# Two f32r matmul halves in one 512-column matmul, and bias loads for v placed further back

## The chip, the cores and the metric

The kernel runs on one core of one Trainium2 chip. The core's engines work side by side: TensorE (PE, with the loads of its stationary operand shown as PEld), VectorE (DVE), ScalarE (ACT), GpSimd (POOL) and SyncE (SP), which here only issues DMAs. Each engine carries out its own instructions in order, and semaphores tie the engines together. The metric is device microseconds of one execution; lower is better.

## The reference

`x` has 256 tokens and 2048 features, float32. A gMLP layer is followed by an attention layer:

```
h = x @ w_in + b_in                      # 2048 x 12288
u, v, g = split(h, 3)                    # 4096 columns each
v = layer_norm(gelu(v)) * vln_g + vln_b
mixed = einsum(causal w_s, v) + b_s      # per 128-token chunk and group of 512
x = layer_norm(ALPHA * x + (gelu(u) * mixed * silu(g)) @ w_out)

k, v = split(x @ kv_w, 2)                # 16 heads of 128
q, gate = split(x @ bw_in, 2)
weights = stick_breaking(q, k)           # strictly causal, in log space
x = layer_norm(ALPHA * x + ((weights @ v) * silu(gate)) @ bw_out)
```

## The kernel before

All products keep float32 accuracy with float32r operands: each operand is split into a high part (a cast on ACT, L89) and a low part (a subtraction on DVE, L90), and `mm3` (L98) adds three matmuls, high by high (L99), high by low (L100) and low by high (L101).

Weights arrive from HBM in chunks of 256 rows by 512 columns (`load_chunk`, L124, 512 KB, issued on SP at L128): six raw buffers (`wraw`), then five buffers each for the high and low parts (`wspl`, `WB = 5`). The order of the instructions on each engine is made by a planner that goes through the program by priority and by its own estimate of when each operand is there; `order(a, b)` fixes that b is issued after a.

**The v part of layer 1** (L385 to L434). v has eight groups of 512 columns. Groups 0 and 1 go through `gemm`. Groups 2 to 7 go in pairs (n = 2, 4, 6) through `bias_block` and `block` (L222), a list of steps from `plan` (L42): products named P1, Q5, P2, P6, P7, Q3, Q4 on sums of quarters, and twelve whole chunks, in the order P1, Q5, P2, chunk, P6, chunk, U3, P7, chunk, chunk, Q3, chunk, chunk, chunk, Q4, five chunks. Counted from 0, step 13 is the seventh chunk and step 14 is Q4. After some steps the accumulated product is added to a tile (`snap`, L321) that starts as a bias broadcast over 128 partitions: `bias_tile` (L378) issues two loads of 256 KB on SP, so that a pair of groups has four. These loads are written at the head of the loop for the pair before (L415). After the loop, `wsr` (the spatial weights, 512 KB) is loaded on SP (L429), masked on POOL (L430) and split on ACT and DVE (L432). The first use of its parts is in the blocks for u and g (L483), whose bias tiles are loaded on POOL's queue (L485).

**Layer 2** (L713). For each j of 4 (four heads each), `gemm` makes v with tokens as rows, 512 columns wide. Then three calls of `gemm_T` make k, q and the gate transposed, with the weight as stationary operand and x as moving one: for each of eight chunks, for each of four heads and two k, three matmuls of 256 columns. Two heads share a PSUM bank; at the end two instructions per bank evacuate it: `split` for k, L726 and L727 for q, Silu (L744) for the gate. Between q and gate, `scores` (L663) makes the logits; `hook` puts the cumulative sums (`weights`, L682) for the first two heads at chunk 3 of the gate's `gemm_T`, and for the other two at chunk 5. `weighted` (L697) follows. PSUM has four banks with the tag `acc` and four with `aux`; the small scratch tiles (`scratch`, L633) come from a pool of three.

Of the kernel before, what the change touches and what calls it, by code (L numbers as in the profile page):

```python
# [9 lines left out]
F32 = mybir.dt.float32  # L10
F32R = mybir.dt.float32r
# [20 lines left out]
WB = 5  # L32
HPINS = {6: (0, 1)}
TAIL = 7
HEAD = 7
ACT_M = (1, 3)
PINS = {4: (0, 1), 5: (2, 3)}
# [4 lines left out]
def plan(nk, hooks={}):  # L42


    each = (nk - 2 * NP) // CK
    steps = ["P1", "Q5", "P2", 1, "P6", 1, "U3", "P7", 1, 1, "Q3"] + [1] * (each - 4) + [0, "Q4"] + [0] * (each - 1)
    return [x for i, s in enumerate(steps) for x in [s, *hooks.get(i, ())]]
# [3 lines left out]
def trunk_kernel(ctx, tc, x, xT, w_in, b_in, vln_g, vln_b, w_sT, b_sT, w_out, kv_w, bw_in, bw_out, ln_g, ln_b, ln_gT, ln_bT, out):  # L51
# [14 lines left out]
    def nm(s):  # L66
        uid[0] += 1
        return f"{s}_{uid[0]}"

    def big_tile(shape, dt, s):  # L70
        return big.tile(shape, dt, tag="big", name=nm(s))
# [16 lines left out]
    def split(hi, lo, src):  # L88
        h = nc.scalar.copy(hi, src)  # L89
        return h, nc.vector.tensor_tensor(out=lo, in0=src, in1=hi.bitcast(F32), op=ALU.subtract)  # L90

    def order(*ins):
        for a, b in zip(ins, ins[1:]):
            tc.add_manual_dep(b.ins, a.ins.name,
                              mybir.DependencyInfo(mybir.DependencyClass.NoSync, mybir.DependencyReason.DATA),
                              reason="issue order")

    def mm3(acc, ah, al, bh, bl, start, stop, **kw):  # L98
        first = nc.tensor.matmul(acc, lhsT=ah, rhs=bh, start=start, stop=False, **kw)  # L99
        nc.tensor.matmul(acc, lhsT=ah, rhs=bl, start=False, stop=False, **kw)  # L100
        nc.tensor.matmul(acc, lhsT=al, rhs=bh, start=False, stop=stop, **kw)  # L101
        return first

    lead.tile([P, P // 8], F32, name="pad")
    xTh = lead.tile([P, KD, S], F32R, name="xTh")
    xTl = lead.tile([P, KD, S], F32R, name="xTl")
    ident = lead.tile([P, P], F32, name="ident")
    ntri = lead.tile([P, P], F32R, name="ntri")
    nones = lead.tile([P, P], F32R, name="nones")
# [14 lines left out]
    def load_chunk(wv, c, col0, spill=False, ahead=None):  # L124
        r = wraw.tile([P, CK, NT], F32, tag="raw", name=nm("raw"))
        src = wv[:, c * CK : (c + 1) * CK, col0 : col0 + NT]
        if not ahead:
            last_w[:] = [nc.sync.dma_start(r, src)]  # L128
        if spill:
            wh, wl = big_tile([P, CK, NT], F32R, "wh"), big_tile([P, CK, NT], F32R, "wl")  # L130
        else:
            wh = wspl.tile([P, CK, NT], F32R, tag="wh", name=nm("wh"))
            wl = wspl.tile([P, CK, NT], F32R, tag="wl", name=nm("wl"))
        if ahead:
            steps = []
            for j in range(CK):
                x_split = ahead(j - CK)
                nc.sync.dma_start(r[:, j, :], src[:, j, :])
                steps += [split(wh[:, j, :], wl[:, j, :], r[:, j, :]), x_split]
            for engine in zip(*steps):  # L140
                order(*engine)
        else:
            split(wh, wl, r)
        return wh, wl
# [174 lines left out]
    def bias_block(w, cols, nk, stat, forms, p, plan, dst, then):  # L319

        def snap(name, acc):  # L321
            d = dst(*dict(P1=(0, 0), Q5=(1, 1), P6=(0, 1), P7=(1, 1))[name])
            snapped[:] = [nc.vector.tensor_tensor(out=d, in0=d, in1=acc, op=ALU.add if name in ("P1", "Q5") else ALU.subtract)]

        def final(tok, half, acc):
            d = dst(tok, half)
            nc.vector.tensor_tensor(out=d, in0=d, in1=acc, op=ALU.add)
            then(tok, half)

        block(w, cols, nk, stat, forms, p, plan, snap, final)  # L330
# [44 lines left out]
        else:  # L375
            load_xT(c * CK, (c + 1) * CK, nc.sync)

    def bias_tile(s, c, q):  # L378
        t = big_tile([P, NTOK, NT], F32, s)
        for tok in range(NTOK):  # L380
            q.dma_start(t[:, tok, :], b_in[c : c + NT].partition_broadcast(P))
        return t


# [2 lines left out]
    for n in range(2):  # L387
# [19 lines left out]
        if n == 0:  # L407
            ahead_v = [bias_tile("v", AW + (n + i) * NT, nc.sync) for i in range(2, 4)]
            xforms = a_forms(xTh[:, 0 : 2 * NP, :], xTl[:, 0 : 2 * NP, :], NP)

    for n in range(2, G, 2):
        pair = ahead_v
        vt += pair
        if n + 2 < G:
            ahead_v = [bias_tile("v", AW + (n + i) * NT, nc.sync) for i in range(2, 4)]  # L415

        def v_then(tok, half, pair=pair, n=n):
            d = pair[1 - half][:, tok, :]
            nc.scalar.activation(d, d, AF.Gelu_apprx_tanh)
            nc.vector.bn_stats(vstats[:, tok, n + 1 - half, :], d)  # L420

        bias_block(w_in, (AW + (n + 1) * NT, AW + n * NT), KD, xstat, xforms, NP, plan(KD),
                   lambda tok, half, pair=pair: pair[1 - half][:, tok, :], v_then)


    wsh = big_tile([P, G, P], F32R, "wsh")
    wsl = big_tile([P, G, P], F32R, "wsl")
    wsr = big_tile([P, G, P], F32, "wsr")
    nc.sync.dma_start(wsr, w_sT.rearrange("g s t -> s g t"))  # L429
    nc.gpsimd.affine_select(out=wsr, in_=wsr, pattern=[[0, G], [1, P]], base=0, channel_multiplier=-1,  # L430
                            compare_op=ALU.is_ge, fill=0.0)
    split(wsh, wsl, wsr)  # L432
    bs = const.tile([P, G], F32, name="bs")
    nc.sync.dma_start(bs, b_sT)  # L434

# [205 lines left out]

    sps, wts = [], []

    def gemm_T(w, col0, evac, hook=None):
        accs = [ps_acc.tile([P, NT], F32, tag="acc", name=nm("acc")) for _ in range(2)]
        wv = w.rearrange("(k p) n -> p k n", p=P)
        for c in range(KD // CK):
            wh, wl = load_chunk(wv, c, col0)
            first = None
            for i in range(HPT):  # L650
                o = accs[i // 2][:, (i % 2) * S : (i % 2 + 1) * S]
                for j in range(CK):
                    k = c * CK + j
                    cs = slice(i * P, (i + 1) * P)
                    m = mm3(o, wh[:, j, cs], wl[:, j, cs], xTh[:, k, :], xTl[:, k, :],
                            start=(k == 0 and i % 2 == 0), stop=(k == KD - 1), **kw)
                    first = first or m
            if hook:
                hook(c, first)
        for i in range(2):  # L660
            evac(slice(2 * i, 2 * i + 2), accs[i].rearrange("p (h t) -> p h t", h=2))

    def scores(i, qT, kT):  # L663
        (qh, ql), (kh, kl) = qT, kT
# [48 lines left out]
    for j in range(4):  # L713
        v = big_tile([P, NTOK, NT], F32R, "avh"), big_tile([P, NTOK, NT], F32R, "avl")
        gemm(kv_w, D + j * NT, KD, xstat, lambda tok, acc, v=v: split(v[0][:, tok, :], v[1][:, tok, :], acc),
             head=HEAD if j == 0 else 0, after=anchor)
        if j == 0:
            sps += [padded("sph"), padded("spl")]
            wts += [(padded("wth"), padded("wtl")) for _ in range(HPT // 2)]
        kT = big_tile([P, HPT, S], F32R, "kTh"), big_tile([P, HPT, S], F32R, "kTl")  # L720
        gemm_T(kv_w, j * NT, lambda i, acc, kT=kT: split(kT[0][:, i, :], kT[1][:, i, :], acc))
        qT = big_tile([P, HPT, S], F32R, "qTh"), big_tile([P, HPT, S], F32R, "qTl")

        def evac_q(i, acc, qT=qT):
            h, l = qT[0][:, i, :], qT[1][:, i, :]
            nc.scalar.mul(h, acc, SCALE)  # L726
            nc.vector.scalar_tensor_tensor(out=l, in0=acc, scalar=SCALE, in1=h.bitcast(F32), op0=ALU.mult, op1=ALU.subtract)  # L727

        gemm_T(bw_in, j * NT, evac_q)
        if j == 0:  # L730
            for m in ACT_M:
                (g, b), r = gb0[m], rt[m]
                for t, op in ((g, ALU.mult), (b, ALU.add)):
                    nc.vector.tensor_tensor(out=r, in0=r, in1=t.unsqueeze(1).to_broadcast([P, NTOK, NT]), op=op)
        pre = nc.scalar.preload_act_table_set("natural_log_exp_and_others")
        tc.keep_in_program_order(pre)
        zz = [scores(i, qT, kT) for i in range(HPT // 2)]

        def hook(c, first, zz=zz):
            if c in CUMSUM:  # L740
                weights(*zz[CUMSUM[c]], CUMSUM[c], first)

        sg = big_tile([P, HPT, S], F32, "sg")
        gemm_T(bw_in, D + j * NT, lambda i, acc, sg=sg: nc.scalar.activation(sg[:, i, :], acc, AF.Silu), hook)  # L744
        z2h, z2l = big_tile([P, HPT, S], F32R, "z2h"), big_tile([P, HPT, S], F32R, "z2l")
        z2s.append((z2h, z2l))
        for i in range(HPT // 2):
            weighted(i, v, sg, z2h, z2l)
        if j == 0:
            z2forms = a_forms(z2h, z2l, NP)  # L750
# [63 lines left out]
```

## Time and profile before

| | us |
|---|---|
| median of 3 runs (1211.24 to 1213.0) | 1211.6 |
| the profiled execution | 1212.62 |
| its span, first to last instruction | 1210.9 |
| PE busy | 1193.0 |
| DVE busy | 856.3 |
| ACT busy | 630.4 |
| POOL busy | 61.5 |

The profiled execution took 1.7 us more than its span, and 1.0 us more than the median. The busy time of an engine is the union of its instructions' times; the shown durations of matmuls overlap, so the time that one matmul really costs is read from start to start.

### The profile page before, as it was taken

To read this page: it belongs to the slowest core of one execution; us is meant where nothing else is said; L and a number is where in the kernel's file an instruction comes from. 1 tells how busy PE (TensorE), PEld (TensorE's weight loads), DVE (VectorE), ACT (ScalarE), POOL (GpSimd) and SP (SyncE) were. 2 spreads that over 40 slices of the span, in tenths; PEclk is the share of its full clock that TensorE was granted. 3 is DMA by queue.
4 is the path that set the end of the run, shared out by engine and by line. 5 is a ranking of instruction groups with operands and counts; after the bars stand their busy time and mean duration, and the time that the engine had idled before them with its cause. 6 is when DMAs were issued, how large, how long until landed. Compare 5 with 4: busy or idle time off the path is not lost.

```text
span 1210.9 us, 16753 instructions
## 1 busy us (share of the span) xinstructions
PE 1193.0 (99%) x6519; PEld 1040.9 (86%) x6519; DVE 856.3 (71%) x950; ACT 630.4 (52%) x712; POOL 61.5 (5%) x110
## 2 busy tenths in 40 slices
PE   8989999999999999999999999999999999999996
PEld 6878888888888888888888889998998999999885
DVE  6968879889889889896554677456455455548665
ACT  6545456656556556565333545474365365456440
POOL 0010001011011010011000000010010000003000
PEclk9989999999999999999999999999999999999998
DMA  9795476677677677678655745545545554555741
GB/s 348 264 289 182 155 248 205 206 249 232 192 236 247 198 232 237 203 247 293 211 193 192 231 150 174 188 148 173 188 158 160 189 160 158 188 174 167 251 157 70
DMA packets 125839, 246.49 MB, mean 204 GB/s; under 512 B 8480, under 2 KB 12096, under 8 KB 125760
## 3 DMA queue, kind: packets, MB, share of 16 engines
q1 hardware_dynamic: 119712, 226.26, 56.2%
q0 software_dynamic: 5760, 18.90, 6.0%
q8 instruction: 51, 0.84, 0.3%
q10 hardware_dynamic: 288, 0.26, 0.1%
q14 instruction: 28, 0.23, 0.1%
HBM read 243.29 MB, written 2.10 MB: 203 GB/s over the span
## 4 chain that ended last, share of the span: by engine, by line
PE 95%; issue 2%; DVE 1%; DMA 1%; ACT 0%; SPq 0%; POOL 0%; DVEq 0%; ACTq 0%; POOLq 0%
PE acc L100 30%; PE acc L101 30%; PE acc L99 30%; DMA raw<-in_w_in 1%; PE ztp L472 1%; PE zp L688 0%; PE op L101 0%; PE op L99 0%; PE zp L101 0%; PE zp L100 0%; PE zp L99 0%; PE op L100 0%; PE zp L691 0%; DVE wl L90 0%; DVE raw L240 0%
## 5 line engine op out<-in xcount | busy, mean ns | idle before, releaser
L90 DVE TENSOR_TENSOR wl<-raw,wh 128x1024 fp32r<-128x1024 f32 (+1 forms) x456 | 552.2, 1223 | 297.4 <-ACT wh L89 295.0
L89 ACT CAST wh<-raw 128x1024 fp32r<-128x1024 f32 (+1 forms) x456 | 474.2, 1049 | 486.7 <-PE acc L101 253.1
L100 PE MATMUL acc<-wl,xTh 128*128 128x512 f32 x786 | 307.6, 392 | 0.8 <-DVE wl L90 0.7
L99 PE MATMUL acc<-wh,xTh 128*128 128x512 f32 x786 | 303.9, 393 | 3.9 <-ACT wh L89 2.4
L101 PE MATMUL acc<-wh,xTl 128*128 128x512 f32 x786 | 306.9, 391 | 0.0
L100 PE MATMUL acc<-xTl,wh 128*128 128x256 f32 x768 | 217.3, 283 | 0.0
L99 PE MATMUL acc<-xTh,wh 128*128 128x256 f32 x768 | 217.2, 283 | 0.0
L101 PE MATMUL acc<-xTh,wl 128*128 128x256 f32 x768 | 217.1, 283 | 0.0
L99 PEld LDWEIGHTS acc<-wh,xTh 128*128 128x128 f32 x786 | 148.3, 189 | 36.3 <-ACT xTh L89 3.2
L100 PEld LDWEIGHTS acc<-wl,xTh 128*128 128x128 f32 x786 | 148.7, 189 | 32.1 <-DVE wl L90 1.7
L101 PEld LDWEIGHTS acc<-wh,xTl 128*128 128x128 f32 x786 | 148.4, 189 | 31.1
L99 PEld LDWEIGHTS acc<-xTh,wh 128*128 128x128 f32 x768 | 147.1, 192 | 0.2
L100 PEld LDWEIGHTS acc<-xTl,wh 128*128 128x128 f32 x768 | 147.1, 192 | 0.2
L101 PEld LDWEIGHTS acc<-xTh,wl 128*128 128x128 f32 x768 | 147.0, 192 | 0.0
L100 PE MATMUL acc<-wl,zh 128*128 128x512 f32 x246 | 95.9, 390 | 0.0
L101 PE MATMUL acc<-wh,zl 128*128 128x512 f32 x246 | 95.7, 389 | 0.0
L99 PE MATMUL acc<-wh,zh 128*128 128x512 f32 x246 | 95.7, 390 | 0.0
L240 DVE TENSOR_TENSOR raw<-raw,raw 128x1024 f32<-128x1024 f32 x52 | 63.7, 1226 | 2.1 <-DMA raw<-in_w_in 0.9
L100 PEld LDWEIGHTS acc<-wl,zh 128*128 128x128 f32 x246 | 46.2, 188 | 9.5
L101 PEld LDWEIGHTS acc<-wh,zl 128*128 128x128 f32 x246 | 46.2, 188 | 9.5
L99 PEld LDWEIGHTS acc<-wh,zh 128*128 128x128 f32 x246 | 46.2, 188 | 9.5
L100 PE MATMUL acc<-wl,z2h 128*128 128x512 f32 (+1 forms) x134 | 48.8, 364 | 0.0
(159 smaller groups left out, 1035.2 us busy)
## 6 DMA issues: line engine op xcount, KB each, us to landing
raw<-in_w_in SPq DMA_DIRECT2D x191, 512.0 KB, 5.3
raw<-in_w_out SPq DMA_DIRECT2D x64, 512.0 KB, 4.6
raw<-in_kv_w SPq DMA_DIRECT2D x64, 512.0 KB, 3.6
raw<-in_bw_in SPq DMA_DIRECT2D x64, 512.0 KB, 3.5
raw<-in_bw_out SPq DMA_DIRECT2D x32, 512.0 KB, 4.5
g<-in_b_in POOLq DMA_DIRECT2D x16, 256.0 KB, 6.7
u<-in_b_in POOLq DMA_DIRECT2D x16, 256.0 KB, 10.3
v<-in_b_in SPq DMA_DIRECT2D x12, 256.0 KB, 7.0
```

What stands on the lines that cost most here:

```text
L89: h = nc.scalar.copy(hi, src)
L90: return h, nc.vector.tensor_tensor(out=lo, in0=src, in1=hi.bitcast(F32), op=ALU.subtract)
L99: first = nc.tensor.matmul(acc, lhsT=ah, rhs=bh, start=start, stop=False, **kw)
L100: nc.tensor.matmul(acc, lhsT=ah, rhs=bl, start=False, stop=False, **kw)
L101: nc.tensor.matmul(acc, lhsT=al, rhs=bh, start=False, stop=stop, **kw)
L240: nc.vector.tensor_tensor(out=dst, in0=dst, in1=src, op=ALU.add)
L472: nc.tensor.transpose(out=tp[:, (kk * NTOK + tok) * P : (kk * NTOK + tok + 1) * P], in_=gt[:, tok, c : c + P], identity=ident)
```

## The change

In `gemm_T`, the high and low parts of x lie side by side in one tile (`xT2`), so that the stationary high part of a weight meets both in one matmul of 512 columns; the low part of the weight meets the high part of x in 256 columns as before. The result is two partial sums in one bank for each head, four banks a call: k takes the `aux` banks, q and the gate `acc`. The first five chunks go chunk by chunk, the last three (`LAST = 3`) head by head. Each head is evacuated by itself: ACT copies the second partial sum to a scratch tile, DVE adds the first, and the former evacuation follows on 256 columns. The hook that was at chunk 5 is called after the first head of the last three chunks.

In the v part, the bias loads for the next pair move from the head of the loop to behind step 14 of the block (`next_v`), and are ordered after the last weight load issued by then; in the last block the load, mask and split of `wsr` stand in the same place. The diff (the evacuations of q and the gate, which follow the one of k, are cut):

```diff
-    xTh = lead.tile([P, KD, S], F32R, name="xTh")
-    xTl = lead.tile([P, KD, S], F32R, name="xTl")
+    xT2 = lead.tile([P, KD, 2, S], F32R, name="xT2")
+    xTh, xTl = xT2[:, :, 0, :], xT2[:, :, 1, :]
...
-    def bias_tile(s, c, q):
+    def bias_tile(s, c, q, after=None):
         t = big_tile([P, NTOK, NT], F32, s)
         for tok in range(NTOK):
-            q.dma_start(t[:, tok, :], b_in[c : c + NT].partition_broadcast(P))
+            d = q.dma_start(t[:, tok, :], b_in[c : c + NT].partition_broadcast(P))
+            if after:
+                order(after, d)
...
+    wsh = big_tile([P, G, P], F32R, "wsh")
+    wsl = big_tile([P, G, P], F32R, "wsl")
     for n in range(2, G, 2):
-        pair = ahead_v
+        pair = list(ahead_v)
         vt += pair
-        if n + 2 < G:
-            ahead_v = [bias_tile("v", AW + (n + i) * NT, nc.sync) for i in range(2, 4)]
+
+        def next_v(n=n):
+            if n + 2 < G:
+                ahead_v[:] = [bias_tile("v", AW + (n + i) * NT, nc.sync, after=last_w[0]) for i in range(2, 4)]
+            else:
+                wsr = big_tile([P, G, P], F32, "wsr")
+                order(last_w[0], nc.sync.dma_start(wsr, w_sT.rearrange("g s t -> s g t")))
+                nc.gpsimd.affine_select(out=wsr, in_=wsr, pattern=[[0, G], [1, P]], base=0, channel_multiplier=-1,
+                                        compare_op=ALU.is_ge, fill=0.0)
+                split(wsh, wsl, wsr)
...
-        bias_block(w_in, (AW + (n + 1) * NT, AW + n * NT), KD, xstat, xforms, NP, plan(KD),
+        bias_block(w_in, (AW + (n + 1) * NT, AW + n * NT), KD, xstat, xforms, NP, plan(KD, {14: [next_v]}),
...
-    def gemm_T(w, col0, evac, hook=None):
-        accs = [ps_acc.tile([P, NT], F32, tag="acc", name=nm("acc")) for _ in range(2)]
+    def gemm_T(w, col0, pool, evac, hook=None):
+        accs = [pool("acc") for _ in range(HPT)]
         wv = w.rearrange("(k p) n -> p k n", p=P)
-        for c in range(KD // CK):
-            wh, wl = load_chunk(wv, c, col0)
+        nch = KD // CK
+        chunks = [None] * nch
+
+        def use(c, i):
+            wh, wl = chunks[c]
             first = None
-            for i in range(HPT):
-                o = accs[i // 2][:, (i % 2) * S : (i % 2 + 1) * S]
-                for j in range(CK):
-                    k = c * CK + j
-                    cs = slice(i * P, (i + 1) * P)
-                    m = mm3(o, wh[:, j, cs], wl[:, j, cs], xTh[:, k, :], xTl[:, k, :],
-                            start=(k == 0 and i % 2 == 0), stop=(k == KD - 1), **kw)
-                    first = first or m
+            for j in range(CK):
+                k = c * CK + j
+                cs = slice(i * P, (i + 1) * P)
+                m = nc.tensor.matmul(accs[i], lhsT=wh[:, j, cs], rhs=xT2[:, k, :, :], start=(k == 0), stop=False, **kw)
+                first = first or m
+                nc.tensor.matmul(accs[i][:, 0:S], lhsT=wl[:, j, cs], rhs=xTh[:, k, :], start=False, stop=(k == KD - 1), **kw)
+            return first
+
+        for c in range(nch - LAST):
+            chunks[c] = load_chunk(wv, c, col0)
+            first = [use(c, i) for i in range(HPT)][0]
             if hook:
                 hook(c, first)
-        for i in range(2):
-            evac(slice(2 * i, 2 * i + 2), accs[i].rearrange("p (h t) -> p h t", h=2))
+        for c in range(nch - LAST, nch):
+            chunks[c] = load_chunk(wv, c, col0)
+        for i in range(HPT):
+            first = [use(c, i) for c in range(nch - LAST, nch)][0]
+            if hook:
+                hook(nch - LAST + i, first)
+            t = scratch("half", S)[:, 0, :]
+            nc.scalar.copy(t, accs[i][:, S : 2 * S])
+            evac(i, accs[i][:, 0:S], t)
...
-        gemm_T(kv_w, j * NT, lambda i, acc, kT=kT: split(kT[0][:, i, :], kT[1][:, i, :], acc))
+
+        def evac_k(i, acc, t, kT=kT):
+            nc.vector.tensor_tensor(out=t, in0=acc, in1=t, op=ALU.add)
+            split(kT[0][:, i, :], kT[1][:, i, :], t)
+
+        gemm_T(kv_w, j * NT, aux, evac_k)
...
-        gemm_T(bw_in, j * NT, evac_q)
+        gemm_T(bw_in, j * NT, acc_bank, evac_q)
...
+        gemm_T(bw_in, D + j * NT, acc_bank, evac_g, hook)
```

## Rows read from the trace of the kernel before

**Rows 1.** The page, part 4: chain that ended last, share of the span by engine.

```profile
PE 95%; issue 2%; DVE 1%; DMA 1%; ACT 0%; SPq 0%; POOL 0%; DVEq 0%; ACTq 0%; POOLq 0%
```

**Rows 2.** Stretches: busy us (instructions) of PE, PEld, DVE, ACT, POOL; clock, DMA share, GB/s.

```profile
68.00:72.00 4.00, 1.36 (x4) 0.82 (x5) 3.04 (x3) 4.00 (x5) 1.95 (x4) 0.84 0.82 266
72.00:76.00 4.00, 4.00 (x11) 3.13 (x10) 4.00 (x5) 1.66 (x2) 0.00 (x0) 0.50 0.75 137
...
745.00:1113.00 368.00, 368.00 (x2799) 356.71 (x2798) 197.64 (x194) 193.15 (x228) 25.60 (x40) 1.00 0.53 169
```

**Rows 3.** Timeline of PE in gemm_T; start us, us, engine, line, operation, shapes, count.

```profile
840.51 0.28 PE L99 MATMUL acc<-xTh,wh 128*128 128x256 f32 x1
...
842.91 0.28 PE L101 MATMUL acc<-xTh,wl 128*128 128x256 f32 x1
```

**Rows 4.** Timeline of PE in gemm, the v projection.

```profile
818.96 0.39 PE L99 MATMUL acc<-wh,xTh 128*128 128x512 f32 x1
...
823.94 0.39 PE L100 MATMUL acc<-wl,xTh 128*128 128x512 f32 x1
```

**Rows 5.** Timeline of PE, cumulative sums of the attention weights.

```profile
806.41 0.34 PE L688 MATMUL zp<-sph,ntri 128*128 128x384 f32 x1
...
807.58 0.28 PE L99 MATMUL acc<-xTh,wh 128*128 128x256 f32 x1
```

**Rows 6.** Timeline of PE where the width of the matmuls changes.

```profile
838.00 0.28 PE L99 MATMUL acc<-xTh,wh 128*128 128x256 f32 x1
838.11 0.28 PE L100 MATMUL acc<-xTl,wh 128*128 128x256 f32 x1
...
915.42 0.40 PE L100 MATMUL acc<-wl,xTh 128*128 128x512 f32 x1
915.66 0.39 PE L101 MATMUL acc<-wh,xTl 128*128 128x512 f32 x1
```

**Rows 7.** Groups of ACT and DVE, 745 to 1113 us: busy us, mean ns, idle before, releasers.

```profile
L89 ACT CAST wh<-raw 128x1024 fp32r<-128x1024 f32 x119 | 124.8, 1049 | 151.2 <-PE acc L100 117.7 <-PE acc L101 33.1
...
L90 DVE TENSOR_TENSOR wl<-raw,wh 128x1024 fp32r<-128x1024 f32 x119 | 146.8, 1234 | 157.4 <-ACT wh L89 157.4
...
L218 DVE TENSOR_TENSOR af<-ar 128x256 f32<-128x256 f32 x2 | 0.8, 422 | 0.0
```

**Rows 8.** Timeline of PE: first matmul of the Q5 product in each v block.

```profile
53.78 0.39 PE L99 MATMUL acc<-wh,afh 128*128 128x512 f32 x1
...
102.48 0.39 PE L99 MATMUL acc<-wh,afh 128*128 128x512 f32 x1
...
144.64 0.39 PE L99 MATMUL acc<-wh,afh 128*128 128x512 f32 x1
```

**Rows 9.** Timelines of SP (SPq), POOL and ACT, 52 to 70 us.

```profile
52.71 1.89 SPq L381 DMA_DIRECT2D v<-in_b_in  x4
54.64 0.84 SPq L429 DMA_DIRECT2D wsr<-in_w_sT  x1
...
66.77 1.09 POOL L430 TENSOR_SCALAR_AFFINE_SELECT wsr<-wsr 128x1024 f32<-128x1024 f32 x1 [12.47 <-DMA wsr<-in_w_sT]
67.80 1.09 POOL L381 DMA_DIRECT2D g<-in_b_in  x2
...
67.88 1.04 ACT L89 CAST wsh<-wsr 128x1024 fp32r<-128x1024 f32 x1 [9.77 <-POOL wsr L430]
```

**Rows 10.** Timeline of PE, the wait near 68 us.

```profile
69.93 0.73 PE L99 MATMUL acc<-wh,xTh 128*128 128x512 f32 x2 [2.38 <-ACT wh L89]
```

**Rows 11.** Second v block: timelines of ACT and SP, landing times of SP's weight loads.

```profile
110.30 2.00 ACT L89 CAST wh<-raw 128x1024 fp32r<-128x1024 f32 x2 [3.80 <-DMA raw<-in_w_in]
...
100.98 10.01 SPq L128 DMA_DIRECT2D raw<-in_w_in  x5
112.64 7.30 SPq L128 DMA_DIRECT2D raw<-in_w_in  x5
...
DMA to landing us min/median/max: 3.5/4.6/6.1
```

More of the change, by code (lines that the diff above doesn't have):

```diff
@@ L34 @@
 TAIL = 7
+LAST = 3
 HEAD = 7
@@ L420, in v_then @@
             nc.vector.bn_stats(vstats[:, tok, n + 1 - half, :], d)
-        bias_block(w_in, (AW + (n + 1) * NT, AW + n * NT), KD, xstat, xforms, NP, plan(KD),
+        bias_block(w_in, (AW + (n + 1) * NT, AW + n * NT), KD, xstat, xforms, NP, plan(KD, {14: [next_v]}),
                    lambda tok, half, pair=pair: pair[1 - half][:, tok, :], v_then)
[L426 to L432, printed above, removed]
     bs = const.tile([P, G], F32, name="bs")
@@ L720, in trunk_kernel, with evac_q @@
         kT = big_tile([P, HPT, S], F32R, "kTh"), big_tile([P, HPT, S], F32R, "kTl")
-        gemm_T(kv_w, j * NT, lambda i, acc, kT=kT: split(kT[0][:, i, :], kT[1][:, i, :], acc))
+        def evac_k(i, acc, t, kT=kT):
+            nc.vector.tensor_tensor(out=t, in0=acc, in1=t, op=ALU.add)
+            split(kT[0][:, i, :], kT[1][:, i, :], t)
+        gemm_T(kv_w, j * NT, aux, evac_k)
         qT = big_tile([P, HPT, S], F32R, "qTh"), big_tile([P, HPT, S], F32R, "qTl")
-        def evac_q(i, acc, qT=qT):
+        def evac_q(i, acc, t, qT=qT):
             h, l = qT[0][:, i, :], qT[1][:, i, :]
-            nc.scalar.mul(h, acc, SCALE)
-            nc.vector.scalar_tensor_tensor(out=l, in0=acc, scalar=SCALE, in1=h.bitcast(F32), op0=ALU.mult, op1=ALU.subtract)
-        gemm_T(bw_in, j * NT, evac_q)
+            nc.vector.tensor_tensor(out=t, in0=acc, in1=t, op=ALU.add)
+            nc.scalar.mul(h, t, SCALE)
+            nc.vector.scalar_tensor_tensor(out=l, in0=t, scalar=SCALE, in1=h.bitcast(F32), op0=ALU.mult, op1=ALU.subtract)
+        gemm_T(bw_in, j * NT, acc_bank, evac_q)
         if j == 0:
@@ L743, in trunk_kernel, with evac_g @@
         sg = big_tile([P, HPT, S], F32, "sg")
-        gemm_T(bw_in, D + j * NT, lambda i, acc, sg=sg: nc.scalar.activation(sg[:, i, :], acc, AF.Silu), hook)
+        def evac_g(i, acc, t, sg=sg):
+            nc.vector.tensor_tensor(out=t, in0=acc, in1=t, op=ALU.add)
+            nc.scalar.activation(sg[:, i, :], t, AF.Silu)
+        gemm_T(bw_in, D + j * NT, acc_bank, evac_g, hook)
         z2h, z2l = big_tile([P, HPT, S], F32R, "z2h"), big_tile([P, HPT, S], F32R, "z2l")
```

## The prediction

> **What bounds the kernel now.** I read the chain of waits first: it is TensorE (PE) for 95% of the span [rows 1]. A PE-bound kernel can gain in two ways only: less matmul time, or an end to stretches where PE waits or runs at a low clock. The table by stretch says where such stretches are [rows 2]: in the attention stage (745 to 1113 us) PE is busy for all of 368 us at a granted clock of 1.00, with VectorE (DVE) at 54% and ScalarE (ACT) at 52%. But from 68 to 72 us it is busy for 1.36 of 4 us and from 72 to 76 us the granted clock is 0.50, the lower of its two levels (1.2 of 2.4 GHz). So one change to the matmuls of the attention stage, and one to the loads around 40 to 80 us, both touch what sets the end.
>
> **The gemm_T part.** Before, each pair (k, head) takes three 256-column matmuls; after, one of 512 and one of 256. The columns are the same (768), the matmuls one fewer. There are 12 calls of gemm_T (3 for each of 4 j), 16 k and 4 heads: 768 pairs.
>
> What does a matmul cost beyond its columns? I take start to start, since the shown durations overlap. Twenty steps of 256 columns go from 840.51 to 842.91: 0.120 us each [rows 3]. Twenty-two of 512 columns go from 818.96 to 823.94: 0.2264 us each [rows 4]. The 256 extra columns cost 0.1064 us, so each matmul pays about 0.0136 us whatever its width. One matmul fewer saves that: 0.360 - 0.3464 = 0.0136 us a pair, times 768 = 10.4 us.
>
> The trace before doesn't show 512 and 256 columns in turn, so I bound it. Four of 384 and four of 256 in twos take 806.41 to 807.58 = 1.17 us [rows 5]; columns at 0.1064 us per 256 plus 0.0136 us each make 1.17 too, so a change of width costs nothing there. Against it, a 512 just after a stretch of 256s took up to 0.24 us; for it, a 256 just after 512s took 0.11 us [rows 6]. If every 512 took 0.24 us the pair would cost 0.36 and nothing would be saved; if every 256 took 0.11, the pair costs 0.336 and 18 us are saved. I take the row that really alternates, and round 10.4 down for the first of the two bounds: 10.0 us.
>
> The Trainium skill, page "TensorE: Matmul & The Clock Gate", section "Back-to-back issue gap", gives columns over 2.4 GHz plus 2.5 ns for a lone gap at the full clock. By that, one matmul fewer is worth 2.5 ns, 1.9 us over all pairs instead of 10, and the time 8 us longer than the sum below. The trace disagrees for these streams: the fixed part is 13 ns [rows 3, 4].
>
> What gemm_T adds: for each of 48 heads an ACT copy and a DVE add of 128x256, and the evacuations in four pieces of 256 instead of two of 512. An instruction of 128x256 costs 0.42 us on DVE; for ACT, whose cast of four times that takes 1.05 as against 1.23 on DVE, I take the same [rows 7]. Per call that is 8 x 0.42 us, less two evacuations of 512 at some 0.65 (an estimate between 0.42 and 1.05 or 1.23): 2.1 us on each. Twelve calls make 25 us, on engines that are idle for 175 and 170 us of that stage [rows 2]: both go to about 62%. Cost zero while the pieces are hidden, and the new order hides them. The last three chunks run head by head, 6 pairs each = 2.1 us, so heads end 2.1 us apart, and each chain (copy, add, cast, subtract: about 2 us) runs under the next head. Only the last head's chain is exposed. After q, its bank is wanted first by head 3 of the gate's first chunk, 2.1 us on, and the score matmuls of heads 0 and 1 can fill in; after k and gate it has longer still. If that cover fails, it costs 0.5 to 2 us at each of 12 ends.
>
> The head-by-head end also wants chunks 5, 6 and 7 within 2.1 us. Split weights have five buffers, and the casts wait for PE to release one (117.7 + 33.1 of the 151.2 us that ACT idles before them [rows 7]), so they run as far ahead as buffers allow: chunk 7 can be cast when chunk 2 ends, 5.5 us before chunk 5 starts and 6.9 us before its own first use, against 2.3 us for cast and subtract. Then the next call has two buffers (chunks 0 and 1, 5.5 us of PE work) until the last head ends with chunk 5, 1.4 us before the end. Enough. x's two parts in one tile change no instruction's count or size.
>
> **The loads for v.** What is late before: the Q5 products start at 53.78, 102.48 and 144.64 us in the three v blocks [rows 8]. Same work, yet the first block takes 48.70 us and the second 42.16: 6.5 us are lost in the first. Who lost them: the spatial weight (wsr) is issued at 54.64 behind four bias loads of 256 KB [rows 9], its mask on GpSimd (POOL) waits 12.47 us for it, and its cast sits in ACT's queue for 9.77 us, in which no weight chunk is cast. PE's stock of split chunks lasts from 58.1 to 67.6 us (9.4 us), then it waits 2.38 us [rows 9, 10], and the rest of the 6.5 us is the half clock after it.
>
> The change moves wsr past nearly two blocks and ties it, as the second and third set of v's bias loads, behind the weight load of step 13 of blocks 2, 4 and 6. On SP's queue that means 0.84 us (wsr) or 1.9 us (four biases) of issue between the seventh and the eighth of a block's twelve chunk loads. In the clean block the seventh is issued about 110.6 and the eighth at 112.64 [rows 11], so the issue fits in the gap; the eighth chunk is used by PE 27 us after Q5, near 129.7. Even with the 12.1 us that wsr took to land it would be there by 125, and cast and subtracted by 127. The bias tiles themselves get some 20 us until the next block's first snap. ACT may wait for wsr in block 6 too: landing 3.5 to 6.1 us for weights in the clean block, 12 us in the crowded one [rows 9, 11]; a hold of 3 to 5 us is inside the stock of 9.4. On POOL the g and u loads stood behind the mask [rows 9]; they may now come earlier, or behind it near 150 us. The first u/g block has its Q5 near 180 us (144.64 + 42.16 - 6.5), 30 us later. I take the whole 6.5 us; lower bound 0.
>
> **Sum**, against the profiled execution's own 1212.6 (span 1210.9 + 1.7 around it): 1212.6 - 10.0 - 6.5 = 1196.1. That execution lies 1.0 above the median of 1211.6, so the forecast is **1195.1**, and 1193 to 1197.5 as its own range.
>
> **Rivals.**
> - *The first block still stalls* (17%). For it: even in the clean block ACT waits 3.8 us for raw weights in this place [rows 11], and if the g and u loads (1 MB) come up to 54 us, they crowd the same landing. Against: ACT is no longer held by wsr there. A third to all of 6.5 us comes back: 1197.3 to 1201.6.
> - *The pieces at the ends show on PE* (11%). The place is the gate's end: copies, Silu with its table load, the second pair's Exp and casts all meet on ACT within 8.3 us. At 0.5 to 1.5 us at the gate and q ends (8): 4 to 8 us (estimate), 1199 to 1203.
> - *A matmul fewer saves next to nothing* (6%). Each 512 after a 256 takes 0.24 us [rows 6], as if the fixed part went with the columns: only the loads gain, 1205.1. Against it stand the alternating rows [rows 5]. By the 2.5 ns of the Trainium skill, page "TensorE: Matmul & The Clock Gate", section "Back-to-back issue gap", the time would be 1203.2.
> - *No gain at all* (3%): both of the former, 1211.6 give or take 2.
> - *Slower* (5%): chunk 7 is late at every end. If ACT or DVE were held there for more than 4.6 us (6.9 - 2.3), by the pieces or the attention's own work, PE would wait at head 0's third chunk; the waits for PE's buffers speak against it [rows 7]. A wait of 2.4 us led to a loss of 6.5 with the clock [rows 10]; half of that at 12 ends is 40 us, and with the gain of 16.5 the time is 1235. It decides where an end loses 1.4 us.
>
> **How the numbers follow.** Forecast 58%, rivals as above. About 0.2% (2.4 us) is what a measurement here can tell from no change. All but the last two are below 1209: faster 0.92; same 0.03; slower 0.05. The range of 8 in 10 takes the forecast with some of the bounds of the alternation, most of the first rival and most of the second: 1191.5 to 1202.5.
>
> **What would show it.** Right: 128 matmuls a call, start to start 0.227 and 0.120 in turn; the period of a j in the attention stage shorter by about 2.5 us (10.0 / 4); Q5 products 42.2 us apart in all three v blocks; clock 1.00 around 70 us; wsr issued near 146 us (110.6 + 42.2 - 6.5). Wrong: PE rows with idle time before a zp or acc matmul, released by an ACT copy or cast; 0.24 in the 512 rows; a new stretch at clock 0.5.

## The result, and the profile after

The changed kernel takes 1200.05 us (median of 4 runs, 1199.62 to 1200.32) against 1211.42 for the kernel before beside it: 0.9905 of its time, 95% interval 0.9888 to 0.9922, a gain of 11.4 us. The profiled execution took 1200.08 us with a span of 1198.3. It is inside the range of 1191.5 to 1202.5, but 5 us above the forecast and above the forecast's own range of 1193 to 1197.5. One of the six executions of the kernel that moves wsr alone, below, took 2364.03 us and is left out of its ratio.

First the chain that ended last, by engine; [rows 1] had TensorE at 95%:

```profile
PE 98%; DVE 1%; DMA 1%; ACT 0%; SPq 0%; DVEq 0%; issue 0%
```

The table by stretch, columns as in [rows 2]:

```profile
10.00:14.00 4.00, 4.00 (x13) 3.10 (x12) 2.82 (x5) 2.41 (x5) 0.00 (x0) 0.62 1.06 398
...
68.00:72.00 4.00, 4.00 (x20) 3.30 (x19) 3.04 (x3) 2.05 (x2) 0.00 (x0) 1.00 0.80 268
72.00:76.00 4.00, 4.00 (x19) 3.32 (x18) 1.23 (x1) 0.06 (x1) 0.00 (x0) 1.00 0.95 333
734.00:1098.00 364.00, 364.00 (x2060) 318.06 (x2059) 216.13 (x264) 220.24 (x307) 22.49 (x37) 1.00 0.55 172
```

The stall at 68 us and the half clock behind it are gone. In the attention stage PE is busy for all of 364 us at clock 1.00, and DVE and ACT are at 59% and 61%. The first row belongs to the start of this execution: the mean granted clock was 0.62 from 10 to 14 us. It isn't shown to be the change's doing; in the profiles of the twelve kernels of this document the first Q5 starts anywhere from 53.25 to 55.04 us.

All waits of PE in the whole run (us in total, times, longest) are at the start, on x and on the tile of the warm-up matmuls (`wz`):

```profile
PE acc L100 <- ACT xT L90: 2.5, 2, 2.1
PE warm L123 <- DVE wz L120: 2.0, 1, 2.0
```

The queues that the loads for v touch, SP, POOL and ACT, columns as in [rows 9]:

```profile
63.05 1.88 SPq L382 DMA_DIRECT2D v<-in_b_in  x4
...
147.37 0.46 SPq L425 DMA_DIRECT2D wsr<-in_w_sT  x1
...
154.45 1.87 POOL L426 TENSOR_SCALAR_AFFINE_SELECT wsr<-wsr 128x1024 f32<-128x1024 f32 x1 [99.46 <-DMA wsr<-in_w_sT]
156.27 1.09 POOL L382 DMA_DIRECT2D g<-in_b_in  x2
...
156.35 1.05 ACT L90 CAST wsh<-wsr 128x1024 fp32r<-128x1024 f32 x1 [2.24 <-POOL wsr L426]
```

wsr now holds ACT for 2.24 us, where it held it for 9.77 [rows 9].

The timeline of PE: the three Q5 firsts, one stretch of gemm_T in k of j=0, the first cumulative-sum matmul of j=0, one stretch in k of j=1, and the first cumulative-sum matmul of j=1:

```profile
54.48 0.39 PE L100 MATMUL acc<-wh,afh 128*128 128x512 f32 x1
...
96.64 0.39 PE L100 MATMUL acc<-wh,afh 128*128 128x512 f32 x1
...
138.80 0.39 PE L100 MATMUL acc<-wh,afh 128*128 128x512 f32 x1
...
744.71 0.40 PE L663 MATMUL acc<-xT,wh 128*128 128x512 f32 x1
744.95 0.28 PE L665 MATMUL acc<-xT,wl 128*128 128x256 f32 x1
...
746.79 0.40 PE L663 MATMUL acc<-xT,wh 128*128 128x512 f32 x1
...
791.79 0.34 PE L708 MATMUL zp<-sph,ntri 128*128 128x384 f32 x1
...
841.19 0.40 PE L663 MATMUL acc<-xT,wh 128*128 128x512 f32 x1
...
844.37 0.40 PE L663 MATMUL acc<-xT,wh 128*128 128x512 f32 x1
...
889.18 0.34 PE L708 MATMUL zp<-sph,ntri 128*128 128x384 f32 x1
```

Two things are to be seen. The Q5 products are 42.16 us apart both times; before, it was 48.70 and 42.16 [rows 8], so all of the 6.5 us came. And the same pair of instructions runs in two rhythms: six pairs from 744.71 to 746.79 take 2.08 us, **0.3467 us** each; nine pairs from 841.19 to 844.37 take 3.18 us, **0.3533** each. The clock, the shapes and the names of the tiles are the same, and neither stretch has a wait. Averaged over runs of pairs, k and q of j=0 go at 0.3467 (120 intervals), k and q of j=1, 2 and 3 at 0.3532 (127 intervals each), and the gate at up to 0.3533 ahead of its cumulative sums and at 0.347 behind them. The mean over all is 0.3508. A period of j went from 98.98 us (905.39 - 806.41 [rows 5]) to 97.39 (889.18 - 791.79): 1.6 us where 2.5 were forecast. The row of the kernel before:

```profile
905.39 0.34 PE L688 MATMUL zp<-sph,ntri 128*128 128x384 f32 x1
```

### The profile page after: what moved, and what is told of

Same layout as the page of the kernel before. It is cut to its first block, busy times and chain, and to the rows that moved or that the text cites. A ratio compares the mean times of both kernels' runs of the same rounds, so it can differ in the third digit from the quotient of the medians.

```text
span 1198.3 us, 15422 instructions
## 1 busy us (share of the span) xinstructions
PE 1182.5 (99%) x5751; PEld 997.3 (83%) x5751; DVE 872.4 (73%) x1014; ACT 657.5 (55%) x792; POOL 61.8 (5%) x110
## 4 chain that ended last, share of the span: by engine, by line
PE 98%; DVE 1%; DMA 1%; ACT 0%; SPq 0%; DVEq 0%; issue 0%
PE acc L100 24%; PE acc L101 24%; PE acc L102 24%; PE acc L663 15%; PE acc L665 8%; PE ztp L477 1%; DMA raw<-in_w_in 1%; PE zp L708 0%; PE op L102 0%; PE op L101 0%; PE zp L102 0%; PE zp L101 0%; PE op L100 0%; PE zp L100 0%; PE zp L711 0%; PE xtp L602 0%
## 5 line engine op out<-in xcount | busy, mean ns | idle before, releaser
L101 PE MATMUL acc<-wl,xT 128*128 128x512 f32 x786 | 306.5, 390 | 0.0
L100 PE MATMUL acc<-wh,xT 128*128 128x512 f32 x786 | 303.7, 392 | 2.5 <-ACT xT L90 2.5
L102 PE MATMUL acc<-wh,xT 128*128 128x512 f32 x786 | 305.9, 390 | 0.0
L663 PE MATMUL acc<-xT,wh 128*128 128x512 f32 x768 | 270.8, 396 | 0.0
L665 PE MATMUL acc<-xT,wl 128*128 128x256 f32 x768 | 214.4, 280 | 0.0
L100 PEld LDWEIGHTS acc<-wh,xT 128*128 128x128 f32 x786 | 148.1, 189 | 33.9 <-ACT xT L90 3.7
L101 PEld LDWEIGHTS acc<-wl,xT 128*128 128x128 f32 x786 | 148.2, 189 | 30.6
L102 PEld LDWEIGHTS acc<-wh,xT 128*128 128x128 f32 x786 | 147.8, 188 | 31.0 <-DVE xT L91 0.2
L663 PEld LDWEIGHTS acc<-xT,wh 128*128 128x128 f32 x768 | 144.2, 188 | 33.2
L665 PEld LDWEIGHTS acc<-xT,wl 128*128 128x128 f32 x768 | 144.8, 189 | 0.3
L102 PE MATMUL acc<-wh,z2l 128*128 128x512 f32 (+1 forms) x134 | 48.7, 364 | 0.0
L100 PE MATMUL acc<-wh,z2h 128*128 128x512 f32 (+1 forms) x134 | 48.5, 365 | 0.0
```

What stands on the lines that cost most here:

```text
L663: m = nc.tensor.matmul(accs[i], lhsT=wh[:, j, cs], rhs=xT2[:, k, :, :], start=(k == 0), stop=False, **kw)
L665: nc.tensor.matmul(accs[i][:, 0:S], lhsT=wl[:, j, cs], rhs=xTh[:, k, :], start=False, stop=(k == KD - 1), **kw)
```

## The experiments

Each kernel was timed beside the kernel before on the same chip; a ratio is to that one, with its 95% interval.

**Only the loads, only the matmuls.** One kernel has the loads of the change with the old gemm_T, the other the new gemm_T with the old loads.

> Only the loads for v and wsr are moved; gemm_T is the old one. If the 6.5 us of the first v block were the whole of what the loads gave: 1204.9 us, Q5 products 42.2 us apart, attention stage as before (99.0 us a j). Rival, the two parts need each other or the loads gave little: above 1208.

> Only gemm_T is the new one; the loads stand as before. If a pair costs 0.3467 us in one rhythm of the matmuls and 0.3533 in another, about half of the pairs each: 1211.4 - 6.8 = 1204.6 us, first v block still 48.7 us. Rival, the saving is a full 0.0136 us a pair and something of the moved loads took 3 us of it back: 1201.2.

The loads alone: 1206.3 us, ratio 0.9946 (0.9935 to 0.9957), a gain of 6.5 us. Its first two Q5 products on PE:

```profile
54.01 0.39 PE L99 MATMUL acc<-wh,afh 128*128 128x512 f32 x1
...
96.17 0.39 PE L99 MATMUL acc<-wh,afh 128*128 128x512 f32 x1
```

The matmuls alone: 1205.4 us, ratio 0.9941 (0.9927 to 0.9955), a gain of 7.2 us, with a period of j of 97.39 and the same two rhythms. The old stall is there again, on ACT and on PE:

```profile
68.44 1.04 ACT L90 CAST wsh<-wsr 128x1024 fp32r<-128x1024 f32 x1 [10.07 <-POOL wsr L431]
...
70.49 0.74 PE L100 MATMUL acc<-wh,xT 128*128 128x512 f32 x2 [2.68 <-ACT wh L90]
```

So each part works without the other. By the ratios they add up to 13.7 us, where both together gave 11.5 (0.0095 of 1211); the intervals, some 1.5 us to either side, allow for that. The profiles show that nothing is lost between the two: from the first Q5 to the start of the last matmul it is 1145.63 us before, 1139.21 with the loads alone, 1138.69 with the matmuls alone and 1132.25 with both, that is 6.4 and 6.9 us apart and 13.4 together. The rest lies ahead of the first Q5 and in the differences between executions.

**Which load was it?** One kernel moves only wsr, the other only the bias loads.

In the first, this is the hook at step 14 in place of next_v, and the bias loads stay at the head of the block:

```diff
+        def load_ws(n=n):
+            if n + 2 == G:
+                wsr = big_tile([P, G, P], F32, "wsr")
+                order(last_w[0], nc.sync.dma_start(wsr, w_sT.rearrange("g s t -> s g t")))
...
+                split(wsh, wsl, wsr)
```

In the second, next_v loses its else branch, and wsr, its mask and its split stay behind the loop, as before:

```diff
+        def next_v(n=n):
+            if n + 2 < G:
+                ahead_v[:] = [bias_tile("v", AW + (n + i) * NT, nc.sync, after=last_w[0]) for i in range(2, 4)]
```

> As before, but wsr alone goes to behind step 14 of the last v block; v's bias loads stay. If the cast of wsr that holds ACT made the stall: first block 42.2 us, 1204.9. Rival, the bias loads crowd the weights: the stall stays in large part, 1208 to 1211.

> As before, but only v's second and third set of bias loads move; wsr is loaded where it was. If wsr was late because it stood behind the bias loads: it lands within some 7 us, ACT is held for 3 to 5 us, inside PE's stock of 9.4, no stall, 1204.9. Rival, its place in ACT's order is enough: PE waits in the first v block again, 1208 to 1211.

wsr alone: 1207.4 us, ratio 0.9953 (0.9938 to 0.9967), 5.7 us. With the bias loads at their old place, the first block is clean. What its profile is behind the one with all the loads moved lies ahead of the first Q5 (55.04 for 54.01); from there to the last matmul it is 1139.1 us, with all the loads 1139.2:

```profile
55.04 0.39 PE L99 MATMUL acc<-wh,afh 128*128 128x512 f32 x1
...
97.22 0.39 PE L99 MATMUL acc<-wh,afh 128*128 128x512 f32 x1
```

The bias loads alone: 1209.3 us, ratio 0.9971 (0.9960 to 0.9981), 3.5 us. This kernel was meant to leave the stall in the first block, and did not: wsr stands behind the bias loads in SP's order, so tying these to a later weight load took wsr along. It was issued at 108.43, and the first block took 42.16 us here too (54.45 to 96.61). But the raw loads behind it came late for the third block, and PE waited there. Its timelines of SP, POOL, DVE, ACT and PE:

```profile
105.17 1.92 SPq L381 DMA_DIRECT2D v<-in_b_in  x4
...
108.43 1.17 SPq L432 DMA_DIRECT2D wsr<-in_w_sT  x1
...
122.45 1.09 POOL L381 DMA_DIRECT2D g<-in_b_in  x2
...
134.17 2.50 DVE L240 TENSOR_TENSOR raw<-raw,raw 128x1024 f32<-128x1024 f32 x2 [1.26 <-DMA raw<-in_w_in]
...
135.50 2.23 ACT L89 CAST wh<-raw 128x1024 fp32r<-128x1024 f32 x2 [4.82 <-DVE raw L240]
...
144.42 0.47 PE L99 MATMUL acc<-wh,afh 128*128 128x512 f32 x1 [1.38 <-DVE v L323]
...
147.25 0.50 PE L99 MATMUL acc<-wh,xTh 128*128 128x512 f32 x1 [0.97 <-DVE v L323]
```

So wsr held the first block up: with wsr moved and the bias loads left, the block was clean. Whether wsr at its old place would hold ACT as long without the bias loads ahead of it was not tested, since this kernel moved it along. Moving the bias loads gave nothing that shows: the interval of wsr alone overlaps that of all the loads, and the profiles are 0.1 us apart from the first Q5 on. What the last kernel adds is the price of this place: four bias loads, wsr and, behind its mask, the loads of g and u come within 20 us, the four weight loads issued from 118.39 on (L236) take 8.2 to 12.5 us to land, where the kernel with all the loads of the change has 4.8 to 9.7, and PE waits 2.4 us (1.38 + 0.97) in the third block. Which of these loads made the weights late was not separated.

**Does the order of widths set the rhythm?** Three orders of the same matmuls: twos throughout (512, 512, 256, 256 for the two k of a chunk and one head); twos in the first chunk of each call alone; blocks (eight 512s of a chunk's four heads and then its eight 256s, six and six per head in the last three chunks). The second, where hi are the 512s and lo the 256s of a chunk and a head:

```diff
+            hi = [(k, 1) for k in ks]
+            lo = [(k, 0) for k in ks]
+            steps = hi + lo if c == 0 else [s for p in zip(hi, lo) for s in p]
```

> The changed kernel, but in each head and chunk the two 512-column matmuls come first and the two of 256 after them. If the slow rhythm belongs to strict alternation, and twos run as the 384s and 256s of the cumulative sums do: 0.3467 us for every pair, 1200 - 3.2 = 1196.8 us. Rival, each 512 that stands within six matmuls of a change of width pays: 0.3533 for every pair, 1202. Rival, the rhythms stay as they are: 1200.

> The changed kernel, with twos in the first chunk of each gemm_T only; then alternation. If a rhythm, once entered, holds until something other than a pair comes: k and q of all four j run at 0.3467 us a pair, 1200 - 2.5 = 1197.5 us. Rival, alternation falls back to 0.3533 by itself: 1200.

> The changed kernel, with all eight 512-column matmuls of a chunk first and then its eight of 256 (in the last three chunks six and six for each head). If only a change of width costs, it is paid an eighth as often: 0.3467 us a pair, 1196.8 us. Rival, the first six 512s after a change pay 5 ns each, as at the old kernel's changes: 0.3496, 1199.

Twos throughout: 1197.5 us, ratio 0.9878 (0.9864 to 0.9891). The pairs take 0.348 (14 from 839.23 to 844.10), between the two rhythms and nearer to the fast one:

```profile
839.23 0.63 PE L663 MATMUL acc<-xT,wh 128*128 128x512 f32 x2
839.70 0.39 PE L667 MATMUL acc<-xT,wl 128*128 128x256 f32 x2
...
844.10 0.62 PE L663 MATMUL acc<-xT,wh 128*128 128x512 f32 x2
```

Twos in the first chunk alone: **1196.8 us**, ratio 0.9871 (0.9858 to 0.9885). The pairs that alternate now take 0.347 in every j, 0.3467 in k and q: in k of j=1, nine from 841.10 to 844.22. The gate's pairs gained too, which the expectation of 1197.5 had left out. The period of j is 96.49 us (887.70 - 791.21), 2.49 shorter than before:

```profile
791.21 0.34 PE L714 MATMUL zp<-sph,ntri 128*128 128x384 f32 x1
...
841.10 0.40 PE L668 MATMUL acc<-xT,wh 128*128 128x512 f32 x1
...
844.22 0.39 PE L668 MATMUL acc<-xT,wh 128*128 128x512 f32 x1
...
887.70 0.34 PE L714 MATMUL zp<-sph,ntri 128*128 128x384 f32 x1
```

Blocks: 1198.5 us, ratio 0.9886 (0.9870 to 0.9901). Eight pairs take 2.79 us, 0.349 each, the 512s 0.230 (1.84 / 8):

```profile
840.61 2.00 PE L667 MATMUL acc<-xT,wh 128*128 128x512 f32 x8
842.45 1.12 PE L670 MATMUL acc<-xT,wl 128*128 128x256 f32 x8
843.40 1.55 PE L667 MATMUL acc<-xT,wh 128*128 128x512 f32 x6
```

The rival of that expectation held (0.3496 and 1199): of the eight 512s from 840.61 the first five take 0.229 to 0.235 us each, the last three 0.226 to 0.227.

So order alone, with the same matmuls, moves the period by up to 0.9 us a j (97.39 to 96.49), and the forecast's 10.0 us for the matmuls are there to be had: 4 x 2.49. Twos in the first chunk alone beat the changed kernel too (0.9885 at most against 0.9888 at least); from twos throughout they can't be told apart.

**How much of a break is enough?** Twos for one head of the first chunk (4 matmuls), in k calls only (twos is set there alone) and in all calls (without that condition). Against the kernel with twos in the whole first chunk, this line differs:

```diff
-            steps = hi + lo if c == 0 else [s for p in zip(hi, lo) for s in p]
+            steps = hi + lo if twos and c == 0 and i == 0 else [s for p in zip(hi, lo) for s in p]
```

> The first two pairs of each k call alone run 512, 512, 256, 256 (one head of one chunk, 4 matmuls of 128); all other pairs of k, q and gate alternate strictly, as in the changed kernel. If the order at the start of a stream decides its rhythm and nothing later changes it: k and q of j = 1 to 3 fall from 0.3533 to 0.3467 a pair, 6 x 64 x 0.0066 = 2.5 us, the gate's first chunks stay as they were (about 20 pairs a gate at the slow rhythm), and the time is 1197.5. If each stretch of slow pairs has to be broken up anew, as twos in the whole first chunk did: under 0.3 us, 1200.

> Twos (512, 512, 256, 256) only for the first head of the first chunk, in each of the 12 calls; the kernel with twos for all four heads of that chunk took 1196.8. If one such group sets the rhythm: the same, 1196.8 give or take 0.6, all pairs at 0.3467. If the stretch of twos has to be long: between 1197.5 and 1200.

In k only: 1200.3 us, ratio 0.9913 (0.9896 to 0.9929). In all calls: 1199.8, ratio 0.9909 (0.9894 to 0.9923). Neither gains on the changed kernel beyond the intervals: the theory that one group sets the fast rhythm fell. With the break in k only, k and q go at 0.3533 in all four j, in j=0 too, where the changed kernel has 0.3467. With it in all calls, one of the eight k and q streams, q of j=0, goes at 0.3467 (nine pairs from 756.65 to 759.77) and the others at 0.3533 (nine from 852.61 to 855.79):

```profile
756.65 0.39 PE L668 MATMUL acc<-xT,wh 128*128 128x512 f32 x1
...
759.77 0.40 PE L668 MATMUL acc<-xT,wh 128*128 128x512 f32 x1
...
852.61 0.40 PE L668 MATMUL acc<-xT,wh 128*128 128x512 f32 x1
...
855.79 0.40 PE L668 MATMUL acc<-xT,wh 128*128 128x512 f32 x1
```

So in these traces a stream of k and q keeps its rhythm until something breaks it. A break of 4 matmuls was followed by either rhythm, one of 16 by the fast one in all eight streams.

**What covers the pieces at the ends?** Only the last chunk goes head by head, so each head has 2 pairs (0.7 us) behind its pieces, not 6.

```diff
-LAST = 3
+LAST = 1
```

> The changed kernel with LAST = 1: heads end 0.7 us apart instead of 2.1, so the evacuation chains of about 2 us stack up at the end. If the cover by the next head is what hides them: PE waits 0.5 to 2 us after q, 1202 to 1208. Rival, the next call's matmuls and the score matmuls hide them anyway: 1200, give or take 1.5 for the rhythm.

1203.2 us, ratio 0.9922 (0.9909 to 0.9934): 2.1 us slower than the changed kernel by the ratios, though the two intervals overlap (0.9909 against 0.9922). PE's waits, and one of the three with the cumulative sums of the second pair of heads ahead of it:

```profile
PE acc L100 <- DVE half L772: 1.4, 3, 0.5
```

```profile
804.24 0.51 PE L708 MATMUL zp<-sph,ntri 128*128 128x384 f32 x2
...
807.07 0.28 PE L102 MATMUL op<-wth,avl 128*128 128x256 f32 x1
807.81 0.47 PE L100 MATMUL acc<-wh,xT 128*128 128x512 f32 x1 [0.46 <-DVE half L772]
```

L772 is the gate's add. The waits are at the gate's end in j=0, 1 and 2, where the next v stream wants the bank; none is behind k or q. The shorter cover is not the only difference: the second pair's cumulative sums, at 797.83 in the changed kernel, now start at 804.24, so that their Exps on ACT (805.97 and 806.86) come on either side of the gate's last copies (806.35). This run doesn't tell the two apart.

## Why the prediction was right, and where it was off

**PE as the bound, and no wait in place of the old one: right.** PE waits for 4.5 us in 1198, all at the start.

**The loads, 6.5 us: right in size and in mechanism.** wsr held ACT; moved alone it gave 5.7 us back (interval 4.0 to 7.5), and with the bias loads 6.5. It was issued at 147.37, forecast near 146; it held ACT for 2.24 us, forecast 3 to 5. The loads of g and u came behind the mask, as the second of the two ways given. The rival in which the first block still stalls fell with 42.16 us in that block. The time alone would not have told: 1200.05 lies in the range of that rival (1197.3 to 1201.6) and in that of the pieces at the ends (1199 to 1203), and neither of the two happened.

**The matmuls, 10.0 us forecast, 6.8 measured: the mis-sized term.** The last matmul of the kernel starts 12.68 us earlier than before (1186.73 for 1199.41, the rows below), and the first transpose ahead of the attention stage starts 5.84 us earlier (703.70 for 709.54); 6.84 us lie between. The step that failed is "I take the row that really alternates". Those rows [rows 5] go in twos, eight matmuls long, and strict alternation over 128 pairs can settle into another rhythm. Twos kept the forecast's rate nearly (0.348 for 0.3464); strict alternation has 0.3467 and 0.3533, and the kernel got both. With 0.3467 everywhere the whole term came, 10.0 us. Both bounds set beside it, 0.336 and 0.36, held; the range took in some of what lies between them, beside most of the first two rivals, and so holds the measured time. The last matmul, before and after:

```profile
1199.41 0.28 PE L101 MATMUL acc<-wh,z2l 128*128 128x256 f32 x1
...
1186.73 0.28 PE L102 MATMUL acc<-wh,z2l 128*128 128x256 f32 x1
```

By the gap of an isolated matmul that the Trainium skill gives, page "TensorE: Matmul & The Clock Gate", section "Back-to-back issue gap", a matmul fewer would give back an estimated 2.5 ns a pair. Against 0.360 [rows 3] the pairs gave back 13.3 ns in the one rhythm and 6.7 in the other, so the measurement decides against that price for these streams in either.

**The pieces at cost zero: right in size; the room behind the gate was misjudged.** The groups of ACT (734 to 1113 us) and DVE (734 to 1098 us), columns as in [rows 7]:

```profile
L680 ACT COPY half<-acc 128x256 f32<-128x256 f32 x48 | 17.7, 369 | 23.0 <-PE acc L665 22.8
...
L694 ACT ACT_TABLE_LOAD x4 | 5.1, 1283 | 0.1
...
L743 DVE TENSOR_TENSOR half<-acc,half 128x256 f32<-128x256 f32 x16 | 6.8, 423 | 7.6 <-ACT half L680 7.6
```

The copy takes 0.37 us and the add 0.42; 0.42 was forecast for both. The engines came to 61% and 59% for the forecast 62%. ACT's new share includes eight more table loads than before (L694 and L695, four each, 1.28 us), which the sum did not have and which cost PE nothing. "After k and gate it has longer still" does not hold for the gate: with `LAST = 1`, the gate's end was the only one that showed. How much of that is the shorter cover and how much the later cumulative sums stays open.

**The base.** The sum made 1196.1 for the profiled execution, which took 1200.08. Of the 4.0 us, 3.2 are the matmuls, and 0.7 is a later first Q5 (54.48 for 53.78 [rows 8]), which is within what the start differs by between the profiles (53.25 to 55.04).

## What to carry to other kernels

Price a stream of matmuls by rows with the same order of widths over the same length; a few rows in another order give the fixed part, but not the rhythm that a long stream settles into. Where two widths take turns, count start to start over some ten pairs in each stage, and try another order of the first chunk: here 16 reordered matmuls of a call's 128 were worth 3 us of 1200. Before tying a load to a later place on a queue, list what stands behind it there: here the bias loads took wsr along, to a place where the next block's weights came late.

## What the hardware showed that was not expected

One alternation of a 512- and a 256-column matmul, each with weights of its own, has two steady rhythms at clock 1.00 without any wait, 0.3467 and 0.3533 us a pair. A stream keeps its rhythm over more than 100 pairs, and from k on into q. Sixteen matmuls in twos at the start of each call gave the fast one in every call; four did not. In the starts to the nanosecond, the fast rhythm of k in j=0 of the changed kernel is pairs of 350 and 344 ns in turn, the slow one of j=1 pairs of 350, 361 and 349 ns over and over. What inside TensorE holds either stays open: the records show starts and nothing between them. Nor do the runs tell a matmul's fixed part from that of its weight load, as each matmul has one (6519 of each before, 5751 after). A 512-column stretch that follows 256s runs at 0.230 us over its first eight, where a long stretch has 0.2264 [rows 4].
